# A hybrid attention and state-space layer: loads of the attention raised to the weights' priority, and the silu of the gate path taken in two halves in weight buffers

## The chip, the cores and the metric

The kernel runs on one core of a Trainium2 chip. The metric is the device time of one execution in microseconds (us), the median of the runs that were made. Beside the runs there is one execution taken with the hardware profiler; the rows shown below are from that one.

The core has a matrix engine (PE in the profile, its weight load PEld), a vector engine (DVE), an activation engine (ACT), a general engine (POOL) and a synchronisation engine (SP). In this kernel every DMA is issued on SP, one after the other, in the order of the program.

## The reference

One decoder layer with 1024 tokens of width 2048, all in fp32. `h` is the normalised and modulated input, `proj = h @ w_in` is cut into eight pieces, two mixers work on them, each has a silu gate path, and a merge and an output product follow.

```python
h = _ln(x) * (1.0 + scale[:, None, :]) + shift[:, None, :]
proj = h @ w_in[i]
q, kv, ng, za, us, zb, ga, gb = jnp.split(proj, offs, axis=-1)
o_a = _nsa(q, kv, jax.nn.sigmoid(ng), rel_bias, ...) * jax.nn.silu(za)
o_b = _s5(us, ...) * jax.nn.silu(zb)
m = jax.nn.sigmoid(ga) * (o_a @ w_branch_nsa[i]) + jax.nn.sigmoid(gb) * (o_b @ w_branch_ssm[i])
y = m @ w_out[i]
x = _ln(DEEPNORM_ALPHA * x + gate[:, None, :] * y) * ln_g[i] + ln_b[i]
```

`_nsa` is attention with 16 heads in 4 groups over 8 blocks of 128 queries; each block looks at compressed keys, at chosen blocks of keys (`ks`) and at a window of keys (`kw`). `_s5` is a diagonal state-space layer. `zb`, the gate of the second mixer, is the piece that `ev_silu` finishes.

## The kernel before, in words

**Products.** Every fp32 matrix is held as a sum of two fp32r parts, high and low, and each product is three matmuls: high by high, low by high, high by low. A weight of 128 x 512 is loaded on SP into a tile `wraw` (`w_unit`, L109, DMA at L114), ACT casts it to `whi` (L119), DVE subtracts to get `wlo` (L121). The tag `wraw` has WR = 2 buffers; `whi` and `wlo` have 3 each.

**The dense phase.** `dense` makes the first pieces of `proj`, mixed with the first attention. Then `seven` (L457) makes the others with a scheme of seven block products for eight, for a pair of weight columns at a time, first for one half of the contraction (half 1, results stored to `pt_d`), then for the other (half 0, `pt_d` loaded again at L464 into the two result tiles of the pair). Its weights come from the generator `weights` (L423): four tiles `wb` are loaded (L430), `s3 = a11 - a21` goes into a tile `ws` (L433, L434), which takes a buffer of tag `wraw`, and further sums are made in place in the `wb` tiles (L436, L438, L441). The first product of a pair uses `a11` as loaded, the second uses `a22 - s3`. The generator is drawn under high priority. Each product's result is added into the two result tiles by DVE (L469). These are from the pool of stage tiles, 128 x 1024, tag `stg`, four buffers.

When a pair of half 0 is complete, its result goes through `ev_tanh` (pieces `ga`, `gb`) or `ev_silu` (piece `zb`, the last four pairs). `ev_silu` (L343) takes a third stage tile, writes tanh(y / 2) into it on ACT (L345, 128 x 1024), multiplies on DVE (L346, 128 x 1024) and stores (L347).

**Attention.** The first five query blocks of each of the four groups (20 units) run early, between the dense products; the other 12 units run after the dense phase, between the products of `branch_nsa`. At the first unit of a group `Attention.group` (L979) loads its keys and values: window keys `kw`, `ks` (L990), `bn`, `vc`, `bf`, `vw`, `vs`, with four small memsets on DVE. `Attention.unit` (L1036) loads the block's queries `q` (L1044 to L1046, two DMAs into the two halves of the partitions) and then computes scores (`scores`, L1032). In the early attention `q`, `ks` and `kw` have one buffer each, in the second two. The first call of `group` is at L620, the second attention's own call is elsewhere.

**Second attention and `branch_nsa`.** 16 tiles `op` are loaded from `oa_d` (L632, L633) and `product` (L671 to L673) multiplies them with `w_bn`, whose weights come through `w_unit` and so through tag `wraw`, under high priority.

**Order.** The program is written in one order, and a scheduler gives each engine its own order by the priorities of the instructions: `tc.high_priority(offset=WPRI)`, WPRI = 300, moves what is issued inside it ahead of ordinary work by so many steps. An engine runs its list strictly in order. A tile's buffer is handed on when the last reader of its former tile has run.

The tags and buffers that matter:

```python
raw = (rp or wp).tile([128, 512], F32, name="wraw", tag="wraw", bufs=3 if rp else WR)
s3 = wp.tile([128, 4, 128], F32, name="ws", tag="wraw", bufs=WR)
WPRI = 300
PS_, PT, PWB, WR = 3, 2, 4, 2
```

Of the kernel before, what the change touches and what calls it, by code (L numbers as in the profile page):

```python
# [5 lines left out]
F32 = mybir.dt.float32  # L6
F32R = mybir.dt.float32r
I32 = mybir.dt.int32
AF = mybir.ActivationFunctionType
# [4 lines left out]
ADD, SUB, MUL, MAX, MIN = ALU.add, ALU.subtract, ALU.mult, ALU.max, ALU.min  # L14
# [10 lines left out]
WPRI = 300  # L25
PS_, PT, PWB, WR = 3, 2, 4, 2
# [5 lines left out]
def hybrid_kernel(tc, A, out):  # L32
    with ExitStack() as es:
        _hybrid(es, tc, A, out)
# [17 lines left out]
def _hybrid(es, tc, A, out):  # L52
    nc = tc.nc
    V, S, P, PE = nc.vector, nc.scalar, nc.gpsimd, nc.tensor
    ld, st_ = nc.sync.dma_start, nc.sync.dma_start
    rd = nc.sync.dma_start
# [6 lines left out]
    def scratch(name, shape):  # L63
        return dp.tile(shape, F32, name=name)
# [6 lines left out]
    k_d = [[scratch(f"k_d{w}_{g}", [2, 64, T]) for g in range(G)] for w in range(2)]  # L71
    v_d = [[[scratch(f"v_d{w}_{g}_{hf}", [128, 4, 128]) for hf in range(2)] for g in range(G)] for w in range(2)]
# [7 lines left out]
    kcc_d = scratch("kcc_d", [128, G, 64])  # L80
# [12 lines left out]
    ident = cst.tile([128, 128], F32, name="ident")  # L93
# [3 lines left out]
    gts = cst.tile([128, NB, 48], F32, name="gts")  # L97
# [4 lines left out]
    wp = es.enter_context(tc.tile_pool(name="wp", bufs=3))  # L102
# [33 lines left out]
    def stage(dt=F32):  # L136
        return stp.tile([128, T], dt, name="stg", tag="stg")
# [12 lines left out]
    lh, rh = slice(0, 512), slice(512, 1024)  # L150
# [190 lines left out]
        st_(dst, y)  # L341

    def ev_silu(y, dst):  # L343
        s = stage()
        S.activation(s, y, AF.Tanh, scale=0.5)  # L345
        V.scalar_tensor_tensor(y, s, 1.0, y, op0=ADD, op1=MUL)  # L346
        st_(dst, y)  # L347

    def dense_ng():
# [214 lines left out]
    late_jobs = [(TILES["ga"][i], ev_tanh, ga_d[i]) for i in range(16)]  # L564
    late_jobs += [(TILES["gb"][i], ev_tanh, gb_d[i]) for i in range(16)]
    late_jobs += [(TILES["zb"][i], ev_silu, zb_d[i]) for i in range(8)]
    pairs = [late_jobs[i:i + 2] for i in range(0, 40, 2)]

# [17 lines left out]
    with tc.tile_pool(name="cp", bufs=1) as cp:  # L586
# [1 line left out]
    dense_ng()  # L588
    pss_cm.__exit__(None, None, None)

    env = dict(nc=nc, A=A, ld=ld, rd=rd, st=st_, ident=ident, gts=gts, k_d=k_d, v_d=v_d, kcc_d=kcc_d,
               vcc_d=vcc_d, q_d=q_d, za_d=za_d, tz_d=tz_d, bf_d=bf_d, oa_d=oa_d)
    late = [(g, qb) for g in range(G) for qb in range(EARLY[g], NB)]

# [10 lines left out]
    def step():  # L605
        nonlocal n
        fn, *a = work[n]
        n += 1
        with tc.high_priority(offset=WPRI if fn is fetch_h else 0):
            fn(*a)  # L610

    with tc.tile_pool(name="at", bufs=1) as ap, tc.tile_pool(name="aps", bufs=1, space=PSUM) as aps:
        att = Attention(env, ap, aps, 0, max(EARLY), dict(pw=2, psl=2, pt=2, s=2, t=1, o=1))
        early = [(g, qb) for g in range(G) for qb in range(EARLY[g])]
        grp = None
        for u, (g, qb) in enumerate(early):
            if g != grp:
                while n < n_group[g]:
                    step()
                att.group(g)  # L620
                grp = g
            att.unit(qb)
            while n < (u + 1) * (len(work) - 8) // len(early):
                step()
# [124 lines left out]
    with (tc.tile_pool(name="at2", bufs=1, side="right") as ap,  # L749
          tc.tile_pool(name="opx", bufs=16, side="right") as opx, tc.tile_pool(name="aps2", bufs=1, space=PSUM) as aps):  # L750
        att = Attention(env, ap, aps, min(qb for _, qb in late), NB, dict(pw=PWB, psl=4, pt=3, s=PS_, t=PT, o=1, q=2, pc=2, k=2))
# [201 lines left out]
class Attention:  # L953
# [82 lines left out]
    def unit(self, qb):  # L1036
        nc, g = self.nc, self.g
        V, S, PE, P = nc.vector, nc.scalar, nc.tensor, nc.gpsimd
        rd, st_ = self.rd, self.st

        def f(ap):
            return ap.bitcast(F32)

        q = self.tl("q", [128, 8, 128], F32R, "q")  # L1044
        for i in range(2):
            rd(f(q)[64 * i:64 * i + 64], self.q_d[g][:, :, 128 * qb:128 * qb + 128])  # L1046
        za = self.tl("za", [128, 2, 128], F32, "q")
        for i in range(2):
            rd(za[:, i], self.za_d[2 * g + i][:, 128 * qb:128 * qb + 128])
# [205 lines left out]
        c = slice(128 * (qb % 4), 128 * (qb % 4) + 128)  # L1255
# [399 lines left out]
```

## Time and profile before

| what | value |
|---|---|
| median of 3 runs | 3156.6 us (3153.21 to 3157.78) |
| profiled execution, own time | 3153.5 us |
| its span on the core | 3151.6 us |
| mean granted TensorE clock | 0.979 of full speed |
| PE busy | 3019.9 us, 96% of the span |
| DVE busy | 2028.3 us, 64% |
| ACT busy | 1224.7 us, 39% |
| chain that ended last, by engine | PE 84%, DMA 8%, DVE 4%, ACT 2% |

The chain that ended last is followed back from the last instruction, each time to what released it; its shares tell where the time of the program lies. An engine's busy time alone doesn't, since engines work beside each other. A matmul's start is what the profile is sure of; its end is modelled. The granted clock is the share of the full rate of 2.4 GHz that PE was given in a stretch; it goes between two levels, 1.2 and 2.4 GHz, so a value of 0.75 means that half of the stretch was at the lower one.

### The profile page before, as it was taken

The numbers are of one execution on the slowest core, as the hardware profiler recorded it, in microseconds if no ns is written. First come the engines' busy times: TensorE is split into PE (matmuls) and PEld (weight loads), VectorE is DVE, ScalarE is ACT, GpSimd is POOL, SyncE is SP. The second block draws the span as 40 slices with busy tenths as digits, with TensorE's granted clock in tenths as the row PEclk, the third lists the DMA queues.
The fourth block names the chain that finished last, engine by engine and source line by source line (L and its number), as shares of the span: only waits on it lengthen the run. The fifth ranks groups of instructions, "written<-read, shape, count | busy, mean of one in ns | idle before, by whom it ended". The sixth has DMA issues, their size and how long they took to land.

```text
span 3151.6 us, 43574 instructions
## 1 busy us (share of the span) xinstructions
PE 3019.9 (96%) x15069; PEld 2463.3 (78%) x15069; DVE 2028.3 (64%) x5245; ACT 1224.7 (39%) x2469; POOL 36.3 (1%) x36
## 2 busy tenths in 40 slices
PE   7999999999999999999999999999999998999897
PEld 4467788887888788878877888778888886788685
DVE  8444678763576377657667777768776667534645
ACT  4212222222344254435445544346554445323421
POOL 0000000000000000000000000000000000000000
PEclk9999999999999999999989999999999999999898
DMA  9854524345464643334465544576785451635835
GB/s 361 306 174 152 176 89 141 96 127 136 126 196 159 198 136 110 102 107 128 166 244 168 159 144 148 177 217 195 233 260 163 138 180 57 233 117 183 286 124 174
DMA packets 332758, 534.58 MB, mean 170 GB/s; under 512 B 45940, under 2 KB 145460, under 8 KB 332536
## 3 DMA queue, kind: packets, MB, share of 16 engines
q1 hardware_dynamic: 332536, 531.79, 52.5%
q8 instruction: 119, 1.95, 0.3%
q14 instruction: 103, 0.84, 0.1%
HBM read 384.58 MB, written 150.50 MB: 170 GB/s over the span
## 4 chain that ended last, share of the span: by engine, by line
PE 84%; DMA 8%; DVE 4%; ACT 2%; issue 1%; SPq 1%; DVEq 0%; ACTq 0%
PE dps L131 8%; PE dps L449 7%; PE dps L451 7%; PE dps L450 7%; PE dps L132 7%; PE dps L134 7%; PE po L1175 4%; PE ps L1032 4%; PE pt L1153 3%; PE pa L672 3%; PE pa L671 3%; PE pa L673 3%; PE e L804 2%; PE e L805 2%; PE e L803 2%; DMA q<-q_d 1%
## 5 line engine op out<-in xcount | busy, mean ns | idle before, releaser
L119 ACT CAST whi<-wraw 128x512 fp32r<-128x512 f32 x376 | 232.1, 619 | 740.0 <-PE dps L132 327.0
L121 DVE TENSOR_TENSOR wlo<-wraw,whi 128x512 fp32r<-128x512 f32 x376 | 259.6, 692 | 324.1 <-ACT whi L119 305.1
L449 PE MATMUL dps<-hhi,whi 128*128 128x512 f32 x960 | 384.8, 401 | 8.8 <-DVE stg L469 8.2
L450 PE MATMUL dps<-hlo,whi 128*128 128x512 f32 x960 | 379.2, 395 | 0.0
L451 PE MATMUL dps<-hhi,wlo 128*128 128x512 f32 x960 | 376.3, 397 | 0.1
L131 PE MATMUL dps<-hhi,whi 128*128 128x512 f32 x792 | 316.2, 399 | 5.1 <-ACT whi L119 4.4
L132 PE MATMUL dps<-hlo,whi 128*128 128x512 f32 x792 | 312.9, 395 | 0.0
L119 ACT CAST whi<-wb 128x512 fp32r<-128x512 f32 x240 | 148.5, 619 | 292.1 <-PE dps L450 173.0
L134 PE MATMUL dps<-hhi,wlo 128*128 128x512 f32 x792 | 256.1, 396 | 0.0
L1157 ACT CAST pth<-pt 128x512 fp32r<-128x512 f32 (+1 forms) x320 | 165.7, 531 | 227.6 <-PE pt L1153 220.8
L1158 DVE TENSOR_TENSOR ptl<-pt,pth 128x512 fp32r<-128x512 f32 (+1 forms) x320 | 196.1, 620 | 88.0 <-ACT pth L1157 85.8
L469 DVE TENSOR_TENSOR stg<-dps,stg 128x512 f32<-128x512 f32 x280 | 188.6, 686 | 73.7 <-PE dps L451 62.7
L449 PEld LDWEIGHTS dps<-hhi,whi 128*128 128x128 f32 x960 | 182.5, 190 | 46.6 <-issue 7.0
L672 PE MATMUL pa<-op,whi 128*128 128x512 f32 x528 | 209.2, 396 | 4.9 <-DMA op<-oa_d 4.3
L671 PE MATMUL pa<-op,whi 128*128 128x512 f32 x528 | 209.0, 398 | 3.1 <-DVE mn L1060 1.9
L451 PEld LDWEIGHTS dps<-hhi,wlo 128*128 128x128 f32 x960 | 182.2, 190 | 37.7 <-DVE wlo L121 0.9
L450 PEld LDWEIGHTS dps<-hlo,whi 128*128 128x128 f32 x960 | 182.6, 190 | 34.8
L673 PE MATMUL pa<-op,wlo 128*128 128x512 f32 x528 | 208.6, 397 | 0.0
L121 DVE TENSOR_TENSOR wlo<-wb,whi 128x512 fp32r<-128x512 f32 x240 | 165.0, 688 | 43.3 <-ACT whi L119 41.9
L131 PEld LDWEIGHTS dps<-hhi,whi 128*128 128x128 f32 x792 | 149.7, 189 | 47.5 <-issue 9.1
L132 PEld LDWEIGHTS dps<-hlo,whi 128*128 128x128 f32 x792 | 149.7, 189 | 30.5 <-issue 1.2
L134 PEld LDWEIGHTS dps<-hhi,wlo 128*128 128x128 f32 x792 | 148.5, 189 | 31.9 <-issue 1.9
(372 smaller groups left out, 6135.7 us busy)
## 6 DMA issues: line engine op xcount, KB each, us to landing
wb<-in_w_in SPq DMA_DIRECT2D x160, 256.0 KB, 3.6
wraw<-in_w_in SPq DMA_DIRECT2D x144, 256.0 KB, 3.7
wa<-in_w_ss SPq DMA_DIRECT2D x64, 512.0 KB, 7.4
wraw<-in_w_out SPq DMA_DIRECT2D x112, 256.0 KB, 3.0
pt_d<-stg SPq DMA_DIRECT2D x40, 512.0 KB, 2.9
stg<-pt_d SPq DMA_DIRECT2D x40, 512.0 KB, 4.4
wg<-in_w_gate SPq DMA_DIRECT2D x32, 512.0 KB, 4.9
q<-q_d SPq DMA_DIRECT2D x64, 256.0 KB, 4.4
```

What stands on the lines that cost most here:

```text
L119: S.copy(hi, raw)
L121: V.tensor_tensor(lo, raw, f(hi), op=SUB)
L131: PE.matmul(ps[hf], hi[:, ku], hx[k][hf][0], start=a, stop=False)
L132: PE.matmul(ps[hf], hi[:, ku], hx[k][hf][1], start=False, stop=False)
L134: PE.matmul(ps[hf], lo[:, ku], hx[k][hf][0], start=False, stop=z)
L449: PE.matmul(ps, hi[:, j], bh, start=first and j == 0, stop=False, skip_group_check=True)
L450: PE.matmul(ps, hi[:, j], bl, start=False, stop=False, skip_group_check=True)
L451: PE.matmul(ps, lo[:, j], bh, start=False, stop=j == 3, skip_group_check=True)
L671: PE.matmul(ps, hi[:, j], x[k][0], start=k == 0, stop=False)
L672: PE.matmul(ps, hi[:, j], x[k][1], start=False, stop=False)
L673: PE.matmul(ps, lo[:, j], x[k][0], start=False, stop=k == 7)
L1158: V.tensor_tensor(lo[0:n, :w], tp[0:n, :w], f(hi[0:n, :w]), op=SUB)
```

## The change

Three things are changed. `group` of the early attention is called under high priority. The load of a unit's `q` is under high priority, in both attentions. `ev_silu` takes no stage tile any more; it goes through the two halves of the result tile, and for each takes a tile `ws` of 128 x 512 from tag `wraw`, writes the tanh of the half into it and multiplies. ACT has 8 instructions more (2094 for 2086), DVE 8 more (5238 for 5230); PE, SP and POOL have as many as before.

```diff
     def ev_silu(y, dst):
-        s = stage()
-        S.activation(s, y, AF.Tanh, scale=0.5)
-        V.scalar_tensor_tensor(y, s, 1.0, y, op0=ADD, op1=MUL)
+        for c in (lh, rh):
+            s = wp.tile([128, 512], F32, name="ws", tag="wraw", bufs=WR)
+            S.activation(s, y[:, c], AF.Tanh, scale=0.5)
+            V.scalar_tensor_tensor(y[:, c], s, 1.0, y[:, c], op0=ADD, op1=MUL)
         st_(dst, y)
...
-    env = dict(nc=nc, A=A, ld=ld, rd=rd, st=st_, ident=ident, gts=gts, k_d=k_d, v_d=v_d, kcc_d=kcc_d,
+    env = dict(nc=nc, tc=tc, A=A, ld=ld, rd=rd, st=st_, ident=ident, gts=gts, k_d=k_d, v_d=v_d, kcc_d=kcc_d,
...
-                att.group(g)
+                with tc.high_priority(offset=WPRI):
+                    att.group(g)
...
-        q = self.tl("q", [128, 8, 128], F32R, "q")
-        for i in range(2):
-            rd(f(q)[64 * i:64 * i + 64], self.q_d[g][:, :, 128 * qb:128 * qb + 128])
+        with self.tc.high_priority(offset=WPRI):
+            q = self.tl("q", [128, 8, 128], F32R, "q")
+            for i in range(2):
+                rd(f(q)[64 * i:64 * i + 64], self.q_d[g][:, :, 128 * qb:128 * qb + 128])
```

The order of PE's matmuls differs at the four group starts of the early attention, and from the start of the fourth group to the end of the second attention; the last part of the program is the same. Three places show how the other engines' lists moved. A number behind a name counts the tiles, so it differs between the two kernels for one and the same thing.

The first place is SP at the switch to the third group (`pt_d` are stores of half 1, `wb` the weights of `seven`). Before:

```order
L502 DMA pt_d67_325<-stg_13113 128x1024
L430 DMA wb_13763<-in_w_in 128x512
L990 DMA ks_11909<-k_d0_2_91 128x640
L1046 DMA q_11928<-q_d2_87 64x8x128 x2
L430 DMA wb_13765<-in_w_in 128x512
L430 DMA wb_13767<-in_w_in 128x512
```

And in the changed kernel:

```order
L503 DMA pt_d67_325<-stg_13113 128x1024
L431 DMA wb_13763<-in_w_in 128x512
L1049 DMA q_11928<-q_d2_87 64x8x128 x2
L992 DMA ks_11909<-k_d0_2_91 128x640
L431 DMA wb_13765<-in_w_in 128x512
L431 DMA wb_13767<-in_w_in 128x512
```

The loads of `q` now stand ahead of the load of `ks`, right behind the same `wb`.

The second place is DVE at the border between two pairs of `zb` in half 0. Before, the pairs' result tiles are 18506 and 18507 (second pair), 18655 and 18656 (third), 18804 and 18805 (fourth); `ws_18667` of the third pair stands 20 rows further up, so that here its sums are under way:

```order
L469 TENSOR_TENSOR stg_18507<-dps_18564,stg_18507 128x512
L434 TENSOR_TENSOR ws_18816<-wb_18808,wb_18812 128x512
L469 TENSOR_TENSOR stg_18507<-dps_18545,stg_18507 128x512
L121 TENSOR_TENSOR wlo_18632<-wb_18516,whi_18630 128x512
L469 TENSOR_TENSOR stg_18506<-dps_18524,stg_18506 128x512
L438 TENSOR_TENSOR wb_18812<-wb_18812,wb_18814 128x512
L121 TENSOR_TENSOR wlo_18671<-wb_18659,whi_18669 128x512
L436 TENSOR_TENSOR wb_18659<-wb_18665,ws_18667 128x512
L469 TENSOR_TENSOR stg_18506<-dps_18564,stg_18506 128x512
L121 TENSOR_TENSOR wlo_18692<-wb_18659,whi_18690 128x512
L441 TENSOR_TENSOR wb_18659<-wb_18661,wb_18659 128x512
L346 SCALAR_TENSOR_TENSOR stg_18506<-stg_18647,stg_18506 128x1024
```

In the changed kernel the second pair's result tiles are 18512 and 18513, the third's 18667 and 18668, and `ws_18679` belongs to the third:

```order
L470 TENSOR_TENSOR stg_18512<-dps_18530,stg_18512 128x512
L347 SCALAR_TENSOR_TENSOR stg_18512<-ws_18653,stg_18512 128x512
L347 SCALAR_TENSOR_TENSOR stg_18512<-ws_18656,stg_18512 128x512
L470 TENSOR_TENSOR stg_18513<-dps_18551,stg_18513 128x512
L347 SCALAR_TENSOR_TENSOR stg_18513<-ws_18660,stg_18513 128x512
L347 SCALAR_TENSOR_TENSOR stg_18513<-ws_18663,stg_18513 128x512
L470 TENSOR_TENSOR stg_18667<-dps_18685,stg_18667 128x512
L435 TENSOR_TENSOR ws_18679<-wb_18671,wb_18675 128x512
L470 TENSOR_TENSOR stg_18668<-dps_18685,stg_18668 128x512 x2
L437 TENSOR_TENSOR wb_18671<-wb_18677,ws_18679 128x512
L439 TENSOR_TENSOR wb_18675<-wb_18675,wb_18677 128x512
L121 TENSOR_TENSOR wlo_18704<-wb_18671,whi_18702 128x512
```

Before, the weights of the next pair (L434, L436, L441) stand ahead of the multiplication (L346) that ends the pair; now all four half multiplications (L347) stand ahead of the next pair's `ws` (L435), and three adds of the next pair's first product stand around it.

The third place is SP at the entry into the second attention. Before:

```order
L347 DMA zb_d3_124<-stg_18507 128x1024
L114 DMA wraw_18972<-in_w_bn 128x512
L347 DMA zb_d4_125<-stg_18655 128x1024
L464 DMA stg_18804<-pt_d42_300 128x1024
L464 DMA stg_18805<-pt_d43_301 128x1024
L347 DMA zb_d5_126<-stg_18656 128x1024
L114 DMA wraw_18990<-in_w_bn 128x512
L114 DMA wraw_19013<-in_w_bn 128x512
L114 DMA wraw_19031<-in_w_bn 128x512
L965 DMA selc_18967<-in_sel_const 128x96
L990 DMA ks_19053<-k_d0_0_89 128x1024
L114 DMA wraw_19385<-in_w_bn 128x512
```

And in the changed kernel (`ga_d` is fetched for the merge):

```order
L348 DMA zb_d4_125<-stg_18667 128x1024
L682 DMA stg_19032<-ga_d0_129 128x512
L348 DMA zb_d5_126<-stg_18668 128x1024
L682 DMA stg_19073<-ga_d1_130 128x512
L1049 DMA q_19098<-q_d0_85 64x8x128 x2
L967 DMA selc_18991<-in_sel_const 128x96
L992 DMA ks_19077<-k_d0_0_89 128x1024
L996 DMA bn_19079<-tz_d0_196 128x4x256
L1001 DMA vc_19081<-vcc_d_195 64x128
L114 DMA wraw_18996<-in_w_bn 128x512
L114 DMA wraw_19014<-in_w_bn 128x512
L1001 DMA vc_19081<-vcc_d_195 64x128
```

Before, four loads of `w_bn` stand ahead of `ks` and the first among the stores of `zb`; now `q`, `selc`, `ks`, `bn` and the first half of `vc` stand ahead of the first load of `w_bn`.

## Rows read from the trace of the kernel before

**Rows 1.** Page, parts 1 and 2: busy time of each engine; granted clock in 40 slices.
```profile
PE 3019.9 (96%) x15069; PEld 2463.3 (78%) x15069; DVE 2028.3 (64%) x5245; ACT 1224.7 (39%) x2469; POOL 36.3 (1%) x36
...
PEclk9999999999999999999989999999999999999898
```

**Rows 2.** Table of PE's waits: us in total, times, longest.
```profile
PE dps L449 <- DVE stg L469: 8.2, 8, 6.0
PE ps L1032 <- DMA q<-q_d: 7.3, 4, 3.8
```

**Rows 3.** Timeline of SP at the third group: start, us, instruction, count.
```profile
1386.00 0.60 SPq L990 DMA_DIRECT2D ks<-k_d  x1
1386.66 1.22 SPq L1046 DMA_DIRECT2D q<-q_d  x2
```

**Rows 4.** Timeline of PE at the third group; idle before it in brackets.
```profile
1395.60 1.14 PE L1032 MATMUL ps<-kw,q 128*128 128x192 f32 x4 [3.80 <-DMA q<-q_d]
```

**Rows 5.** Page, part 6: issues, KB each, us from issue to landing.
```profile
q<-q_d SPq DMA_DIRECT2D x64, 256.0 KB, 4.4
```

**Rows 6.** Timeline of PE around 2005 us.
```profile
2003.27 0.39 PE L451 MATMUL dps<-hhi,wlo 128*128 128x512 f32 x1
2009.65 0.77 PE L449 MATMUL dps<-hhi,whi 128*128 128x512 f32 x1 [5.99 <-DVE stg L469]
```

**Rows 7.** Timeline of DVE around 2008 us.
```profile
2008.09 1.42 DVE L469 TENSOR_TENSOR stg<-dps,stg 128x512 f32<-128x512 f32 x2 [3.27 <-DMA stg<-pt_d]
```

**Rows 8.** Windows: busy us (count) by engine, then granted clock, DMA share, GB/s.
```profile
750.00:760.00 10.00, 3.19 (x17) 2.97 (x16) 6.63 (x12) 3.95 (x6) 0.00 (x0) 0.65 0.24 78
760.00:770.00 10.00, 10.00 (x57) 9.38 (x57) 4.23 (x10) 2.70 (x7) 0.00 (x0) 0.84 0.21 64
2000.00:2010.00 10.00, 4.01 (x18) 3.07 (x17) 4.25 (x6) 1.47 (x3) 0.00 (x0) 0.78 1.05 403
2010.00:2020.00 10.00, 10.00 (x40) 8.09 (x40) 5.86 (x9) 1.24 (x2) 0.00 (x0) 0.88 0.31 107
1590.00:1600.00 10.00, 5.74 (x18) 3.50 (x19) 4.52 (x14) 4.96 (x11) 0.00 (x0) 0.63 1.04 372
1600.00:1610.00 10.00, 7.54 (x22) 5.30 (x23) 8.43 (x37) 4.78 (x10) 0.82 (x1) 0.50 1.04 376
1610.00:1620.00 10.00, 9.53 (x43) 7.73 (x42) 7.45 (x21) 2.96 (x6) 0.64 (x2) 0.84 0.43 153
```

**Rows 9.** Groups by form, 1985 to 2062 us: busy, mean ns, idle before.
```profile
L346 DVE SCALAR_TENSOR_TENSOR stg<-stg 128x1024 f32<-128x1024 f32 x7 | 8.6, 1223 | 2.1 <-ACT stg L345 2.1
L345 ACT ACTIVATE stg<-stg 128x1024 f32<-128x1024 f32 x7 | 7.4, 1062 | 5.9 <-DVE stg L469 5.9
```

**Rows 10.** Timeline of DVE, a `wb` of the last silu pair.
```profile
2038.03 0.69 DVE L436 TENSOR_TENSOR wb<-wb,ws 128x512 f32<-128x512 f32 x1
```

**Rows 11.** Timeline of ACT, the cast behind that `wb`.
```profile
2038.84 0.62 ACT L119 CAST whi<-wb 128x512 fp32r<-128x512 f32 x1 [1.73 <-DVE wb L436]
```

**Rows 12.** Timeline of PE, two matmuls eleven starts apart.
```profile
2038.77 0.39 PE L449 MATMUL dps<-hhi,whi 128*128 128x512 f32 x1
...
2041.27 0.39 PE L449 MATMUL dps<-hl,whi 128*128 128x512 f32 x1
```

**Rows 13.** Timeline of PE at the entry into the second attention.
```profile
2083.34 1.29 PE L1032 MATMUL ps<-kw,q 128*128 128x448 f32 x6 [0.53 <-issue]
2086.02 0.47 PE L1032 MATMUL ps<-kw,q 128*128 128x256 f32 x2 [1.38 <-DVE mn L1060]
2088.42 0.77 PE L671 MATMUL pa<-op,whi 128*128 128x512 f32 x1 [1.92 <-DVE mn L1060]
```

**Rows 14.** Tile `wraw`, 2020 to 2090 us: DMA to landing.
```profile
DMA to landing us min/median/max: 2.6/5.5/7.6
```

**Rows 15.** Timeline of SP ahead of the second attention.
```profile
2027.79 0.38 SPq L114 DMA_DIRECT2D wraw<-in_w_bn  x1
...
2045.90 13.76 SPq L114 DMA_DIRECT2D wraw<-in_w_bn  x3
```

## The prediction

> **What bounds the kernel now.** I read the page first, for who is full: PE is busy for 96% of the span, DVE for 64%, ACT for 39%, and the granted TensorE clock reads 9 tenths or more in all but a few slices [rows 1]. The change alters no matmul, so it can only move the 4% in which PE stands still, and the stretches of low clock around them. The table of PE's waits comes second: what the change could take away is the 7.3 us for `q` at the score matmuls and the 8.2 us for DVE's adds into the stage tiles in `seven` [rows 2]. The rest of the views were read at the places where the new order of instructions differs: two group switches of the early attention, the four silu pairs that end the dense phase (half 0), and the entry into the second attention.
>
> A stall of PE costs more than its idle time. At 2003 us PE stops, comes back at 2009.65 [rows 6], and the two windows there show a granted clock of 0.78 and 0.88 [rows 8]: (1 - 0.78) x 10 + (1 - 0.88) x 10 = 3.4 us of full-speed work are lost on top. A longer idle of some 6.8 us at 750 us lost 3.5 + 1.6 = 5.1 us by the same sum; several stops near each other from 1590 us lost 3.7 + 5.0 + 1.6 = 10.3 us [rows 8]. These three prices are used below.
>
> **Loads with priority.** At the switch to the third group SP issued `ks` at 1386.00 for 0.60 us and only then `q` [rows 3], and PE waited 3.80 us for `q` [rows 4]. Now `q` stands ahead of `ks`. Gain: the issue, 1386.66 - 1386.00 = 0.66 us, and the `ks` bytes no longer ahead. The median `q` lands in 4.4 us [rows 5], this one took about 8 (SP 1387, PE 1395.6); of the 3.7 us excess I give `ks` its share of the bytes just issued (320 KB of 2 x 512 + 256 + 320 = 1,600 KB), 0.7 us. Sum -1.4 us. Bounds: nothing gained if the queue's other bytes set it, and -(3.8 + 3.4) = -7.2 us if the stall goes entirely. At the switch to the fourth group the remaining `q` wait is the other half of the 7.3 us, but there PE's order also moves the scores earlier by about as much as `q`: 0, between +1 and -6. The first two groups showed no such wait of size: 0. The two weights that now queue behind the first group's loads are cast only when PE frees a buffer, which covers them.
>
> **Silu in halves, cost by itself.** Eight more ACT and eight more DVE instructions. Full tanh 1062 ns, full DVE op 1223 ns [rows 9]. A half costs at least half of that (0.53, 0.61) and at most a 512-wide operation of the engine (0.62 on ACT [rows 11], 0.69 on DVE [rows 10]); I take 0.60 and 0.65, nearer the wide rows since a fixed part is seldom halved. On engines this idle it costs nothing, except where PE waits behind it. The Trainium skill, "VectorE: DVE Perf Modes", section "The TRN2 errata", speaks against such splitting: an operation that reads SBUF pays a fixed extra time once per instruction. By its figures a half would be 0.69 on DVE and 0.61 on ACT (an estimate), which adds about 0.2 us to the sum below.
>
> **Silu in halves, what it moves.** Here lies the weight. The halves live in the two buffers of tag `wraw`, and so does `ws`, the difference a11 - a21 that every pair's weights start from. Before, `ws` of the next pair was made long before the pair ended. Now its buffer comes free only after the old pair's halves, and DVE's new order says so: all four halves, the next pair's first adds, then `ws`, `wb`. PE can run the next pair's product 1, whose weights are ready; product 2 needs `wb` = a22 - `ws`, cast. From the end of a pair's last matmul: add 0.69, tanh half 0.60, silu half 0.65, first add of the next pair 0.69, `ws` 0.69, two more adds 1.38, `wb` 0.69, cast 0.62 = 6.0 us; four crossings between engines at 0.12 each (`wb` ends at 2038.03 + 0.69, its cast begins at 2038.84 [rows 10, 11]) make it 6.5. PE has 12 matmuls to cover it, at 2.50 / 11 = 0.227 us each [rows 12]: 2.7, less the overlap of the last one, 2.6. Idle 3.9, plus clock 3.4 = 7.3 us, at two boundaries (second to third and third to fourth pair): **+14.6 us**. Bounds: 2 x 3.9 = 7.8 if the clock stays, 2 x 8.7 = 17.4 if the crossings cost four times as much.
>
> At the first boundary the two extra adds aren't between: 6.5 - 1.4 - 2.6 = 2.5 idle + 3.4 clock. There the old stall goes: DVE waited 3.27 us for the reload `stg<-pt_d` [rows 7], PE 5.99 us behind it [rows 6], 9.4 us with the clock. In the new order the first reload is issued ahead of the `op` loads, but the second behind the old pair's stores; I leave 1 us for it. -9.4 + 5.9 + 1.0 = **-2.5 us**, between -9.4 (nothing late) and +1.2 (that reload late by 4.7).
>
> **Entry into the second attention.** Before, `wraw<-in_w_bn` was issued at 2027.79 and three more from 2045.90 [rows 15], 37 us and more ahead of use; PE's stops there sum to 0.53 + 1.38 + 1.92 = 3.8 us [rows 13], with 3.4 of clock 7.2. Now the slots are held by the last silu halves, and SP issues `q`, `ks`, `bn` and `vc` ahead of the first `w_bn`. PE's first work after the last pair is a product that needs it. From the last matmul: a crossing and the add 0.8, tanh 0.60, silu half 0.65 with their crossings 2.3; issue 0.4; landing 5.5 (median; 2.6 to 7.6 [rows 14]); cast 0.62: 8.8 us idle, clock 5.1 as in the longer stall. 13.9 - 7.2 = **+6.7 us** if the old stops vanish in it, between +3 (landing 2.6) and +10 (landing 7.6 and half of the old stops left). Four small memsets stand ahead of the add on DVE; I take them as done beside the last product. The rest of the second attention has the same matmuls in another interleaving: 0, give or take 5.
>
> **Sum.** -1.4 - 2.5 + 14.6 + 6.7 = +17.4 us. The profiled execution took 3153.5 us (span 3151.6 and 1.9 around it), 3.1 below the median 3156.6 of the runs: 3170.9 by the one, 3174 by the other. I forecast **3174 us**.
>
> **Rivals.** *(A) The halves free `ws` in time.* If tanh and the silu half run so early that `wb` is cast before PE leaves product 1 (a chain of 2.6 us or less instead of 6.5), both boundaries cost nothing: -1.4 - 9.4 + 6.7 = -4.1, 3152 us. For it: ACT is idle for long stretches. Against: the chain's own operations sum to 6.0.
> *(B) Faster: the transfers were the true bound.* PE's stops in the places touched end on DMA or what follows one: `q` 7.3 + 2 x 3.4, the reload 9.4, the entry 7.2. If loads issued early land in time everywhere and the silu halves and `w_bn` hide, -30.7: 3126 us. It decides if `ws` and `w_bn` wait less than the 2.6 us that product 1 covers. "DMA: Bandwidth & Descriptors" of the Trainium skill, section "Rules for kernel authors", has the same rule: issue early, wait late. The `q` rows bear it out in part, but here `w_bn` becomes later, not earlier.
> *(C) The stops fall together.* If the clock falls as from 1590 us, each of the four places costs 10.3 instead of 3.4 or 5.1: 2 x 14.2 + (3.5 + 10.3 - 9.4) + (8.8 + 10.3 - 7.2) - 1.4 = +43.3: 3200 us. The pairs lie some 20 us apart, so PE works at length between stops; against.
>
> **How the numbers follow.** Forecast 0.70, A 0.12, B 0.08, C 0.10. About 0.2%, 6.3 us, is what a measurement can tell from no change. A falls within it, B is faster, the forecast and C are slower. The forecast's own range: gains at their best and stalls at their least, -7.2 - 9.4 + 7.8 + 3 = -5.8; stalls at their most, 1.2 + 17.4 + 10 + 5 = +33.6. All ends at once being unlikely, I go from A's 3152 to 3192, leaving out B and C and little else.
>
> **What would show it.** In the new trace PE should stand idle for 2 to 4 us before the second product of three silu pairs, ended by ACT's cast or DVE's `wb`; for 8 to 10 us before the first `pa` product, ended by `wraw<-in_w_bn`; the 5.99 us stop behind `stg<-pt_d` should be gone or small, and the `q` wait at the third group shorter by 1 to 2 us. I am wrong if `ws` is made before the old pair's last half, if `w_bn` lands within the last pair, or if the clock stays at its upper level (2.4 GHz) across the stops.

## The result, and the profile after

The changed kernel took 3173.95 us (median of 5 runs, 3166.44 to 3176.86), the kernel before 3155.7 us beside it: a ratio of 1.0058, with a 95% interval from 1.0044 to 1.0071, some 18 us slower. The forecast was 3174. The profiled execution took 3168.17 us with a span of 3166.4, 14.8 more than the span of before; it was one of the faster ones.

The page, parts 1 and 2, answers to [rows 1]:

```profile
PE 3015.7 (95%) x15069; PEld 2460.1 (78%) x15069; DVE 2024.6 (64%) x5253; ACT 1225.5 (39%) x2477; POOL 36.0 (1%) x36
...
PEclk9999999999999999999989999989999999999998
```

PE does the same 15069 matmuls; what grew is its idle time, by 19.0 us (span less busy time: 150.7 for 131.7), while its busy time fell by 4.2. The table of PE's waits says for what (the first two lines have no counterpart of size before; the last two answer to [rows 2]):

```profile
PE dps L450 <- ACT whi L119: 11.7, 3, 4.3
PE pa L673 <- issue: 10.2, 1, 10.2
...
PE ps L1034 <- DMA q<-q_d: 7.0, 2, 3.7
...
PE dps L450 <- DVE stg L470: 6.4, 12, 1.7
```

The three waits of 11.7 us in all are the three borders between the silu pairs, the 10.2 is the entry into the second attention. The 5.99 us stop behind the reload [rows 6] is gone; of the adds no wait is longer than 1.7.

**The border.** PE's timeline at the border of the second and third pair: the last matmul of the second pair, the last of the third pair's first product (two of its twelve ran ahead of 2024.22), and the first of the third pair's second product.

```profile
2024.22 0.39 PE L452 MATMUL dps<-hhi,wlo 128*128 128x512 f32 x1
...
2026.48 0.39 PE L452 MATMUL dps<-hl,wlo 128*128 128x512 f32 x1
2031.13 0.79 PE L450 MATMUL dps<-hhi,whi 128*128 128x512 f32 x1 [4.26 <-ACT whi L119]
```

DVE's timeline over the same microseconds (L470 add, L347 silu half, L435 `ws`, L437 `wb`):

```profile
2024.64 0.69 DVE L470 TENSOR_TENSOR stg<-dps,stg 128x512 f32<-128x512 f32 x1 [0.49 <-PE dps L452]
2026.08 1.29 DVE L347 SCALAR_TENSOR_TENSOR stg<-ws,stg 128x512 f32<-128x512 f32 x2 [0.75 <-ACT ws L346]
2027.29 0.68 DVE L470 TENSOR_TENSOR stg<-dps,stg 128x512 f32<-128x512 f32 x1
2027.89 0.68 DVE L435 TENSOR_TENSOR ws<-wb 128x512 f32<-128x512 f32 x1
2028.49 1.28 DVE L470 TENSOR_TENSOR stg<-dps,stg 128x512 f32<-128x512 f32 x2
2029.69 0.68 DVE L437 TENSOR_TENSOR wb<-wb,ws 128x512 f32<-128x512 f32 x1
```

and ACT's, two tanh halves and the cast that PE waits for:

```profile
2025.42 1.16 ACT L346 ACTIVATE ws<-stg 128x512 f32<-128x512 f32 x2 [2.07 <-issue]
2030.46 1.22 ACT L119 CAST whi<-wb 128x512 fp32r<-128x512 f32 x2 [3.89 <-DVE wb L437]
```

This is the chain of the prediction with one link more, a second silu half on DVE. From the end of the old pair's last matmul, 2024.22 + 0.39 = 2024.61, to PE's return at 2031.13 it takes 6.5 us, as forecast: the extra half is made up for by operations that follow each other on DVE at 0.60 us, not 0.69. What covers it is shorter: the new pair's first product ends 2.26 us after the old pair's last matmul, not 2.6, since two of its matmuls ran before that. The clock, in windows of one microsecond at the same place:

```profile
2029.00:2030.00 1.00, 0.00 (x0) 0.00 (x0) 1.00 (x3) 0.00 (x0) 0.00 (x0) 0.91 0.85 250
2030.00:2031.00 1.00, 0.00 (x0) 0.00 (x0) 0.98 (x2) 0.54 (x1) 0.00 (x0) 0.50 1.00 410
...
2036.00:2037.00 1.00, 1.00 (x5) 0.83 (x4) 0.00 (x0) 0.00 (x1) 0.00 (x0) 0.68 0.00 0
2037.00:2038.00 1.00, 1.00 (x6) 0.82 (x5) 0.82 (x2) 0.62 (x1) 0.00 (x0) 1.00 0.00 0
```

It falls to its lower level (1.2 GHz) while PE still stands and comes back at 2036.7: 5.6 us of work at half speed, 2.8 us lost by the clock. The half operations measured, by the groups of this stretch:

```profile
L347 DVE SCALAR_TENSOR_TENSOR stg<-ws,stg 128x512 f32<-128x512 f32 x16 | 10.4, 689 | 5.9 <-ACT ws L346 5.8
L346 ACT ACTIVATE ws<-stg 128x512 f32<-128x512 f32 x16 | 9.3, 625 | 22.4 <-DVE stg L470 16.0 <-issue 6.5
```

So two halves cost 1.38 us where the whole cost 1.22 on DVE, and 1.25 for 1.06 on ACT [rows 9]; where they follow each other directly, as in the rows with x2 above, 1.29 and 1.16. I had taken 0.65 and 0.60. The estimate from the Trainium skill, "VectorE: DVE Perf Modes", section "The TRN2 errata" (a fixed extra time once per instruction), 0.69 and 0.61, was the closer one; the trace agrees with it within 0.02.

**The entry.** PE's timeline at the end of the last silu pair, against [rows 13]:

```profile
2075.00 0.39 PE L452 MATMUL dps<-hhi,wlo 128*128 128x512 f32 x1
2085.55 0.76 PE L673 MATMUL pa<-op,whi 128*128 128x512 f32 x1 [10.16 <-issue]
```

The page names no releaser. ACT's cast tells it, and the two weights were issued on SP at 2078.88, after `q`, `ks`, `bn`, where [rows 15] had the first at 2027.79, 33 us ahead of the first `pa` product (its first matmul runs at 2060.31, within the last silu pair, so the weights' lead was smaller than the 37 us that the prediction read):

```profile
2084.84 0.62 ACT L119 CAST whi<-wraw 128x512 fp32r<-128x512 f32 x1 [6.78 <-DMA wraw<-in_w_bn]
```

```profile
2075.42 1.25 SPq L1049 DMA_DIRECT2D q<-q_d  x2
...
2078.88 1.43 SPq L114 DMA_DIRECT2D wraw<-in_w_bn  x2
```

**The second group's start.** The windows at 1080 us, first of before, then of the changed kernel (columns as in [rows 8]); in the second one the granted clock is 0.60 where it was 0.78, and 33 matmuls run where 45 did:

```profile
1080.00:1090.00 10.00, 5.64 (x23) 4.43 (x23) 4.82 (x14) 3.63 (x8) 0.00 (x0) 0.87 1.10 326
1090.00:1100.00 10.00, 10.00 (x45) 8.40 (x44) 2.72 (x13) 3.31 (x12) 0.00 (x0) 0.78 0.13 46
```

```profile
1080.00:1090.00 10.00, 5.09 (x24) 4.17 (x23) 4.43 (x13) 3.53 (x7) 0.00 (x0) 0.89 1.10 315
1090.00:1100.00 10.00, 9.31 (x33) 7.29 (x32) 2.58 (x12) 3.32 (x12) 0.00 (x0) 0.60 0.22 74
```

**Where the time lies.** Lengths of stretches in us between PE's rows that all kernels have: the early attention's first score to the first product of `seven` (A, the second group's start lies in it); the last four tanh pairs (B); the four silu pairs (C); from their last matmul to the first `e<-op` of the second branch (D, entry and second attention). The experiments' columns are explained with them.

| kernel | loads raised | silu's tile, pairs 1-3 / 4 | `ws` | A | B | C | D |
|---|---|---|---|---|---|---|---|
| before | none | stage / stage | wraw | 310.3 | 88.8 | 85.5 | 611.5 |
| changed | all | wraw / wraw | wraw | 313.7 | 90.3 | 97.9 | 610.8 |
| e11, changed again | all | wraw / wraw | wraw | 313.1 | 90.1 | 96.9 | 613.1 |
| e1 | none | wraw / wraw | wraw | 310.2 | 88.8 | 96.7 | 615.0 |
| e2 | all | stage / stage | wraw | 313.9 | 90.5 | 85.7 | 614.4 |
| e3 | all | wraw / stage | wraw | 313.9 | 90.1 | 98.8 | 615.1 |
| e4 | all | stage / wraw | wraw | 313.2 | 90.4 | 88.2 | 616.9 |
| e5 | all | wraw / wraw | hr | 314.3 | 90.1 | 77.8 | 614.4 |
| e6 | none | stage / stage, halves | wraw | 308.6 | 88.8 | 88.4 | 606.7 |
| e7 | groups | stage / stage | wraw | 311.7 | 88.8 | 87.1 | 609.9 |
| e8 | third, fourth group | stage / stage | wraw | 312.6 | 90.4 | 87.2 | 606.5 |
| e9 | none | stage / stage | hr | 310.7 | 88.2 | 79.7 | 609.3 |
| e10 | all | stage / stage | hr | 313.4 | 90.1 | 88.0 | 618.6 |
| e12 | none | wraw / wraw | hr | 310.7 | 88.1 | 76.8 | 612.4 |

Changed minus before: A +3.4, B +1.5, C +12.4, D -0.7; the rest of the span -1.8. Single runs of one kernel differ by some us (before: 3144.5 to 3162.5 in all), so single cells carry a us or two of chance, D more; it is the columns that count. The rest of the span is no constant either: it is 6 to 8 us shorter than before in e11, e1, e9 and e12, 13 to 15 in e5 and e10.

The stretches don't hold quite the same matmuls, since the order differs. A holds 1480, but 1485 where the queries are raised (1484 in e7): five of the dense phase, 1.1 us, that now run behind the first score. B holds 422 before and 429 in the changed kernel, C 345 and 336, D 3179 and 3181. So some 1 us of A's growth and most of B's is work that moved, and C's loss is a little larger than its length says.

### The profile page after: what moved, and what is told of

Same layout as the page of the kernel before. It is cut to its first block, busy times and chain, and to the rows that moved or that the text cites. A ratio compares the mean times of both kernels' runs of the same rounds, so it can differ in the third digit from the quotient of the medians.

```text
span 3166.4 us, 43577 instructions
## 1 busy us (share of the span) xinstructions
PE 3015.7 (95%) x15069; PEld 2460.1 (78%) x15069; DVE 2024.6 (64%) x5253; ACT 1225.5 (39%) x2477; POOL 36.0 (1%) x36
## 5 line engine op out<-in xcount | busy, mean ns | idle before, releaser
L450 PE MATMUL dps<-hhi,whi 128*128 128x512 f32 x960 | 386.5, 403 | 19.0 <-ACT whi L119 11.7
L470 DVE TENSOR_TENSOR stg<-dps,stg 128x512 f32<-128x512 f32 x280 | 188.2, 685 | 97.1 <-PE dps L452 91.0
L673 PE MATMUL pa<-op,whi 128*128 128x512 f32 x528 | 208.9, 398 | 10.4 <-issue 10.2
```

The source lines that it names most:

```text
L450: PE.matmul(ps, hi[:, j], bh, start=first and j == 0, stop=False, skip_group_check=True)
L673: PE.matmul(ps, hi[:, j], x[k][0], start=k == 0, stop=False)
```

## The experiments

The theory, S: the halves and `ws` share the two buffers of tag `wraw`, and that is what costs. Rivals: the raised loads (L), the halving itself (H).

**e1: the silu change alone.** The changed kernel with the edits for priority taken back.

> The silu halves in the weight buffers, without any load raised in priority. Theory S (the weight buffers couple the silu to the next pair's weights): nearly all of the added time stays, +13 to +20 us over the kernel before, with PE idle about 4.3 us before the second product at the borders of pairs 2 to 3 and 3 to 4, and about 10 us before the first product of the second attention. Rival L (the loads raised in priority delay weights and cause the loss): within 3 us of the kernel before, and no idle of 4 us at the borders.

1.0032 (1.002 to 1.0044), 3165.22 us for 3153.26. PE stands for 4.26 us at each of the three borders:

```profile
1996.97 0.50 PE L450 MATMUL dps<-hhi,whi 128*128 128x512 f32 x1 [4.26 <-ACT whi L119]
...
2022.25 0.79 PE L450 MATMUL dps<-hhi,whi 128*128 128x512 f32 x1 [4.26 <-ACT whi L119]
...
2048.61 0.72 PE L450 MATMUL dps<-hhi,whi 128*128 128x512 f32 x1 [4.26 <-ACT whi L119]
```

The loss, some 10 us, is a little below the range expected, and the stops are as S has them (three, where the changed kernel's first is 3.19; C is 96.7). In the trace C and D are 14.7 us longer than before and the span 6.2; the rest is 8.4 shorter (that execution is the fastest of the twelve), so the loss by time is not the price of the stops alone. L is not the main cause.

**e2: the raised loads alone.**

```diff
-        for c in (lh, rh):
-            s = wp.tile([128, 512], F32, name="ws", tag="wraw", bufs=WR)
...
+        s = stage()
...
```

> The loads raised in priority, the silu as it was. Theory S: no loss, between -4 and +2 us against the kernel before: a gain of about 1.5 us each at the third and fourth group, a loss of about 2 us at the second group, and the 6 us stop behind the reload of the stage tile stays. Rival L: +10 us or more.

1.0007 (0.9995 to 1.0018): no gain to be seen, and no loss clear of noise; by the profile A and D are longer. The stop behind the reload is there (4.6 us). L as the main cause falls.

**e3 and e4: which pairs.** The changed kernel, but the tanh of some pairs goes into a stage tile, still in halves (e3: the last pair, `zb_d[6:]`; e4: the first three, `zb_d[:6]`).

```diff
+        whole = stage() if any(dst is d for d in zb_d[6:]) else None
         for c in (lh, rh):
-            s = wp.tile([128, 512], F32, name="ws", tag="wraw", bufs=WR)
+            s = whole[:, c] if whole is not None else wp.tile([128, 512], F32, name="ws", tag="wraw", bufs=WR)
```

> The changed kernel, but the last of the four silu pairs puts the tanh of its halves into a stage tile instead of weight buffers; pairs 1 to 3 as changed. The first weights of the second attention can load early again. If the entry is worth what the prediction gave it (+6.7 us net of what the entry cost before), this kernel is 6 to 10 us faster than the changed one, 3164 to 3168 us by the median. Rival E (the work behind the entry takes the idle time back, as the two traces suggest, which differ by less than 1 us from the last silu product to the end of the second attention): within 2 us of the changed kernel, though the 10 us idle is gone. The idle of 4.3 us at the two borders stays in both.

> The reverse: pairs 1 to 3 put the tanh of their halves into stage tiles, the last pair into weight buffers as changed. No idle of 4.3 us at the borders of the pairs, 10 us idle at the entry into the second attention. If the entry costs what the prediction gave it: +5 to +9 us over the kernel before. Rival E: within 2 us of the kernel before. If the borders were not what costs: as slow as the changed kernel.

e3: 1.0064 (1.0048 to 1.008), not faster than the changed kernel at all, though its entry has no stop of 10 us any more. e4: 1.002 (1.0008 to 1.0033), +6.3 us, C back at 88.2, the stop of 10.57 us at the entry. Taken alone these contradict each other on what the entry costs: nothing in e3; in e4 +6.3 us over the kernel before, 4 over e2, which has early weights (the intervals of e4 and e2 overlap). Column D, read as a square, offers a reading:

| D, us | weights `w_bn` early | late |
|---|---|---|
| second attention's `q` not raised | 611.5, 606.7, 609.9, 606.5, 609.3: mean 608.8 | 615.0, 612.4: 613.7 |
| raised | 614.4, 615.1, 618.6: 616.0 | 610.8, 613.1, 616.9, 614.4: 613.8 |

By the means, late weights cost 5 us, raised queries 7, and both together no more than either; then in e3 freeing the weights would have left the raised queries' loss in view. The first is borne out by PE's idle time in D: 20.1 to 23.7 us in the five kernels with early weights and queries not raised, 25.6 to 27.8 in the six with late weights. The second is not shown. With early weights and raised queries PE idles 21.6 us in e2, 25.2 in e3 and 26.7 in e10, so e2 doesn't differ from the kernels without; the rest is matmuls at the lower clock, 6.8 to 11.4 us lost in these three against 1.7 to 8.8. And by their times e2 and e8, whose queries differ in the first two groups and in the second attention, lie 0.05% apart, 1.6 us, each with an interval of some 0.12% to either side. A part of the difference lies in the middle of the second attention; windows of 100 us at the same place of the program, of before, of the changed kernel and of e3:

```profile
2260.00:2360.00 100.00, 96.93 (x524) 82.24 (x525) 79.71 (x237) 56.63 (x119) 4.49 (x4) 1.00 0.82 259
```

```profile
2275.00:2375.00 100.00, 98.14 (x541) 85.03 (x540) 81.43 (x234) 60.32 (x125) 4.80 (x4) 1.00 0.83 270
```

```profile
2276.00:2376.00 100.00, 94.11 (x504) 79.82 (x503) 72.55 (x225) 55.11 (x117) 4.49 (x4) 0.97 0.73 235
```

After a late entry PE runs this stretch with 1.9 us idle and 541 matmuls; in e3 it idles 5.9, part of it for `op<-ob_d`, and the clock falls for a while (0.97). Whether the raised `q` loads bring that about was not tried.

**e5: one buffer.** The changed kernel, `ws` elsewhere. It takes one of the eight buffers of the `wb` tiles.

```diff
-        s3 = wp.tile([128, 4, 128], F32, name="ws", tag="wraw", bufs=WR)
+        s3 = hr.tile([128, 4, 128], F32, name="ws", tag="hr")
```

> The changed kernel with one edit: the tile ws of a pair's weights takes a buffer of the wb tiles (tag hr) instead of one of tag wraw; the silu halves stay in wraw. Theory S (the shared buffer, not the halving, makes the stops at the pair borders): the 4.26 us stops of PE at the borders of pairs 2 to 3 and 3 to 4 are gone, the 10 us stop at the entry into the second attention stays, and the kernel is 8 to 14 us faster than the changed one, about +5 us over the kernel before. Rival H (the halving itself: eight more instructions on ACT and DVE at the end of a pair): the stops stay, within 3 us of the changed kernel.

0.9954 (0.9936 to 0.9971): 3139.96 us, 14 us faster than before and some 30 faster than the changed kernel. The halves are still in `wraw`, the eight instructions are still there, and no border stop is left. In PE's waits the 11.7 us line is gone; the entry stayed:

```profile
PE pa L673 <- issue: 10.1, 1, 10.1
...
PE ps L1034 <- DMA q<-q_d: 2.5, 1, 2.5
```

H falls, and for the stops S is shown by direct removal. But the edit does more than remove them: of the 27.7 us between the two spans, 20 lie in C (where PE idles 0.8 us for 14.6), some 10 between the first product of `seven` and the last four tanh pairs. That the kernel passes the one before was expected by neither theory.

**e6: halves without the shared buffer.** The kernel before, tanh and multiplication in halves of a stage tile.

> The kernel before, with the silu of all four pairs in two halves that live in a stage tile; no load raised, no weight buffer taken. Theory S: as fast as the kernel before, within 3 us, no stop of PE at the pair borders, none of 8 us or more at the entry. Rival H: +8 us or more.

0.9993 (0.9981 to 1.0004): halving costs nothing that can be seen. H falls a second time.

**e7 and e8: which loads.** e7 raises only `group`, e8 raises groups and queries only for the third and fourth group of the early attention (the edit shown is e8's, against the changed kernel):

```diff
-                with tc.high_priority(offset=WPRI):
+                with tc.high_priority(offset=WPRI if g > 1 else 0):
...
-        with self.tc.high_priority(offset=WPRI):
+        with self.tc.high_priority(offset=WPRI if g > 1 and self.first == 0 else 0):
```

> Only the loads of a group's keys and values raised in priority; queries and silu as before. All four profiles with raised loads lost 2.9 to 3.6 us between the first scores and the start of the second group's first late product (around 1085 to 1105 us), the one without them lost nothing. If the group loads do it (they go ahead of the two weights that the dense product waits for): the stop before the dense product near 1085 us stays at 4.9 to 7 us, where the kernel before had 4.36, and that stretch loses about 3 us. Rival (the queries do it): the stretch is as in the kernel before, within 1 us. In the whole, both within 4 us of the kernel before.

> The loads of keys, values and queries raised in priority only for the third and fourth group of the early attention; silu as before. If the loss of the raised loads lies at the second group's start and their gain at the later two: 1 to 4 us faster than the kernel before, and the stretch around 1085 to 1105 us as before. Rival (the later groups gain nothing): within 1.5 us of the kernel before.

1.0002 (0.9988 to 1.0016) and 1.0002 (0.999 to 1.0015). All seven traces with all queries raised have 313.1 to 314.3 us in A, the six without any raised queries 308.6 to 311.7, e8 312.6. Less the moved matmuls (0.227 us each), that is 312 to 313, 308.6 to 310.8 and 311.5. So the group's loads alone (e7, 310.8) cost nothing that can be told from chance, as the rival had it, and the raised queries about 2. In the traces with all queries raised the clock is low for 10.2 us there, in the seven others for 3.4 or 6.8. The gain at the later groups isn't there: the times are those of the kernel before, and PE's wait for `q` at the third group is 2.64 to 4.41 us with raised queries and 2.98 to 3.80 without, wherever `ws` is in `wraw`.

**e9 and e10: the edit by itself.** `ws` in the `wb` buffers in the kernel before (e9), and with all raised loads (e10).

> The kernel before with one edit: ws of a pair's weights in a buffer of the wb tiles (tag hr); no load raised, silu whole in a stage tile. It asks where the 14 us come from by which the same edit made the changed kernel faster than the kernel before. Theory W (the edit spaces out the wb loads and so unblocks SP for q and for the reload of the stage tiles): the 3 to 4 us wait for q at the fourth group and the 6 us stop behind the reload are gone here too, -10 to -16 us against the kernel before; and with the weights of the second attention loaded early, no stop at its entry, so up to 5 us better still. Rival (it needs the raised loads or the silu in weight buffers): within 4 us of the kernel before.

> The same edit with the raised loads, silu whole in a stage tile. Against the kernel with ws in tag hr and nothing else, the raised loads add what they added to the kernel before: between -2 and +5 us. Against the one with the silu halves in the weight buffers: no 10 us stop at the entry; 0 to 6 us faster if the entry's stop costs in the end, equal within 2 us if the stretch behind takes it back.

e9: 0.9955 (0.9938 to 0.9971), the same 14 us. What theory W expected of the stops came: no wait for `q` is left in the table of PE's waits, and behind the reload none is over 1.42 us; the further 5 us did not. In the trace 6 us of the gain lie in C, 12 between the first product of `seven` and the tanh pairs (769.2 us for 781.3; 768.3 to 769.3 in e5, e10 and e12). That it comes about through SP, as W has it, is not shown. e10: 1.0014 (1.0004 to 1.0024), 18 us behind e9 and e5 alike, which neither theory had. Its C has the stop behind the reload again (5.61 us, C = 88.0), and its D is the longest of all (618.6). e5 differs from e10 by the silu without a stage tile alone, and has no such stop: that part of the change does remove it. Without raised loads (e9) it is gone as well.

**e11: the changed kernel again.**

> The changed kernel as it is, again, for a second trace and for times beside the same runs of the kernel before as the two others: +14 to +22 us; stops of PE of 3.2, 4.26 and 4.26 us at the three borders of the silu pairs and of 9 to 11 us at the entry, unchanged. The stretch from the last silu product to the end of the second attention, which was 0.7 us shorter than in the kernel before in the first trace: if that was chance, +2 to +5 us here; if the stretch takes the stop back, within 1 us.

1.0042 (1.0027 to 1.0058), some 13 us, just below the range expected. Stops of 3.19, 4.26, 4.26 and 9.73 us; D +1.6 against before, between the two expectations.

**e12: the shared buffer and the raised loads out, the silu in halves in.**

> The silu halves in weight buffers with ws in tag hr, and no load raised: what is left of the change if the shared buffer and the raised loads go. If the raised loads cost 3 us at the second group (all seven profiles with raised queries show 10.2 us at the lower clock there, all six others 3.4 or 6.8) and the silu without a stage tile takes away the stop behind the reload: no stop at the pair borders, none of 4 us or more behind the reload, 6.8 us or less at the lower clock near 1100 us, and -14 to -20 us against the kernel before, the fastest of all. Rival (with ws in tag hr the rest of the change is worth nothing either way): within 3 us of the kernel that has ws in tag hr alone, -10 to -16 us.

0.9925 (0.9912 to 0.9939): 3132.17 us for 3155.61, 23 us faster than the kernel before, the fastest of all, and more than either expectation. Where it gains on e9 the traces don't show: their spans are 3135.2 and 3135.0 us, since e12's profiled execution is the slowest of its five. C is 76.8, A is as before. There is no wait for `q` in the table of PE's waits. SP's timeline at the fourth group, before and then e12:

```profile
1634.64 7.56 SPq L430 DMA_DIRECT2D wb<-in_w_in  x3
...
1655.22 1.31 SPq L1046 DMA_DIRECT2D q<-q_d  x2
```

```profile
1630.88 4.92 SPq L431 DMA_DIRECT2D wb<-in_w_in  x3
...
1637.48 1.22 SPq L1047 DMA_DIRECT2D q<-q_d  x2
```

`q` goes out 18 us earlier without any raised priority. It isn't a longer lead: PE's scores of that group start 20 us earlier too (1644.9 for 1664.9), 7.4 us behind the issue for 9.7. The stop of the entry is still there, 8.13 us.

## Why the prediction was right, and where it was not

The direction and the cause of the main term were right. That 3174 and the median 3173.95 agree so closely is luck: the same kernel again (e11) was some 13 us slower than before, not 18, and errors in the parts cancel.

**The borders: the stops right, the clock's price wrong.** Idle of 3.9 us was forecast at two borders, 4.26 measured at both in both traces; 2.5 at the first, 3.19 measured. The chain took the 6.5 us that were forecast; the missing 0.4 is the cover, 2.26 us and not 2.6, because two matmuls of the new pair's first product ran ahead of the old pair's last one. That the shared buffer is the cause is shown by e5 (the buffer away, the stops away) and by e1 and e6 (halves with and without it). The sum for these terms was -2.5 + 14.6 = +12.1; C measured +12.4 and +11.4. But its parts don't match so well. PE is idle for 14.6 us in C (two further stops, of 1.7 and 1.2 us, are in it) against 6.2 before: +8.4. I had 2.5 + 1.0 + 7.8 = 11.3 of idle for it, less the 6.0 of the old stop: +5.3. Matmuls at the lower clock lose 6.1 us against 1.4: +4.7. I had three times 3.4, less 3.4 for the old stop, so +6.8. The step that failed is "3.4 us of full-speed work are lost on top": the sum over (1 - clock) takes in the last part of the stop itself, where PE does nothing and loses nothing. In the kernel before, the clock was low from 2005.7 to 2012.5 us, and PE stood still until 2009.65; the price of that stop was 1.4, so the old stop was worth 7.4 and not 9.4. The idle was put 3.1 too low, the clock 2.1 too high, and nine matmuls left the stretch: the errors cancel.

**The entry: the stop right, the term mis-sized.** 8.8 us were forecast, 10.16 and 9.73 measured. Of the difference the four memsets are 0.8: I had put them beside the last product, and DVE ran them ahead of the add that the stop waits for. But the net of +6.7 isn't in the traces of the changed kernel (D -0.7 and +1.6). The idle is: 26.4 us in D in both, against 20.5 before, +5.9. What failed is the clock's price of this term, 5.1 less 3.4, and "the rest of the second attention: 0, give or take 5": over all of D the changed kernel's matmuls lose 4.5 and 6.6 us at the lower clock, those of the kernel before 8.8, the most of the five kernels in its cell of the square. The entry's stop itself loses 2.9 us in the matmuls behind it (the clock is low until 2091.3), the old stops there lost 3.0. By the means of the square the changed kernel pays 5.0 for D, near the 6.7, but single traces of one cell differ by as much.

**The raised loads: wrong by some 4 us.** The forecast was -1.4 in all; e2 measured about +2, not clear of zero. The -1.4 at the third group isn't there: the wait for `q` shrank from 3.80 to 3.39 and 2.64 us, but was 2.98 and 3.42 in two kernels without raised loads as well. The first two groups were put at 0, "no such wait of size"; A grew by 3.4 and 2.8, of which some 2.3 and 1.7 are loss at the second group's start. With its scores moved ahead PE stops a second time, 0.69 us, right behind the 4.91 us stop for `whi`, and works longer at the lower clock (the windows above). The 1.5 that the tanh pairs are longer is mostly the seven matmuls more that run there. The "DMA: Bandwidth & Descriptors" page of the Trainium skill, section "Rules for kernel authors", has it that a DMA is best issued early. Here the raised queries gained nothing in eight traces: at the third group `q` went out ahead of `ks` alone, and the wait there was 2.64 to 4.41 us in the six of them with `ws` in `wraw`.

**The rivals.** A needed a chain of 2.6 us; it was 6.5. A part of what B needed did appear in e5, e9 and e12, the stops behind the reload and at the borders gone, but only with `ws` out of the way, and in e5 and e12 the stop for `w_bn` stayed. C did not occur: the border stops began 26 us apart, and the clock recovered between them.

What stays open: whether raised queries lengthen the second attention at all and what the entry's stop costs in the end, how much of the gain of e5, e9 and e12 ahead of the tanh pairs comes from SP's order and how much from the weights themselves, and where e12 gains on e9.

## What to carry to other kernels

Before a temporary is put into a tag with two buffers, list who else rotates through them: a buffer at the end of one pipeline stage that the next stage's first step also needs can turn a hidden operation into a serial chain. Price such a chain link by link against the work that covers it; here that gave the border's stop to 0.4 us. Removing a stop may not return its time (e3), so undo parts in pairs as well as alone, and before a stretch's length is read as a loss, see whether it holds the same work in both kernels.

## What the runs showed that was not expected

One line, the tag of a 128x512 tile, was worth 14 us in the kernel before and some 30 in the changed one. And the same raised loads cost about 2 us with `ws` in one tag (e2 against before, not clear of zero), 18 in the other (e10 against e9), and 9 there with the silu in weight buffers (e5 against e12, 0.9954 and 0.9925): with an order that a scheduler makes anew for each edit, a part's price is only good beside the parts it was measured with. The clock was mostly seen to fall while PE still stood, so a stop's price is read from the matmuls behind it and not from the mean clock of a window that holds the stop.
